# Turning the FFN's gated products by transposing DMAs, and splitting weight units in one piece

## The chip, the cores and the metric

The kernel runs on one core of a Trainium2 chip. The metric is the device time of one execution in microseconds (us). Before the change the median of three runs is 935.49 us (934.88 to 937.68). Engines are named as in the profile: PE multiplies matrices, DVE and ACT work on vectors, POOL does a few small things, SP issues the DMAs.

## The reference, cut to what matters

The program is a trunk of two layers over 256 tokens with 1024 channels in fp32. Each layer has a mixing part (gated linear attention beside grouped-query attention), then a SwiGLU feed-forward network (FFN), then an embedding step. The part that the change touches is this:

```python
gate, up = jnp.split(rms_norm(h, g_ffn_pre) @ w_ffn_in, 2, axis=-1)   # 256 x 2816 each
h = h + rms_norm((jax.nn.silu(gate) * up) @ w_ffn_out, g_ffn_post)
```

The gated product `silu(gate) * up` has 2816 columns. It is the left operand of the second product, so it has to stand with its columns on the partitions: it must be turned (transposed) before PE can use it.

## The kernel before, in words

**Precision.** Every fp32 operand of a matmul is split into a high and a low part of type fp32r, and a product is three matmuls, high by high, high by low, low by high (`mm3`, line 96; `times`, line 536, has the same three). A matmul takes 128 rows of contraction and 512 columns.

**Weights.** They come as *units* of four 128x512 blocks (2048 columns; 2112 in the first projection), in one fixed order, `plan`. `Stream` (line 208) loads a unit by a DMA on SP's queue into a buffer of the pool `raw` (two buffers), splits it into `wh` and `wl` (four buffers each) and hands it out in order. `fill` splits ahead as long as fewer than `depth` (4, for a while 3) units are held; `take` hands out the oldest of the list `ready`; `done` gives a unit back, starts the next load and splits the next unit. `put` (line 263) cuts a unit into `parts` pieces, by default two of 1024 columns, and `split` (line 108) does each piece with one ACT cast for the high part and one DVE subtraction for the low part.

**The FFN.** The 2816 columns are 11 blocks of 256. Blocks 0 and 1 are done for each half of the tokens at the start (four gated products of 128x256 in all, from line 1224). Blocks 4, 5 and 10 (`PLAIN`) are done one by one (`block`, line 1239; 128 tokens x 256 columns for both halves of the tokens, side by side in one 128x512 tile). Blocks 2 and 3, 6 and 7, 8 and 9 (`PAIRS`) are done by a scheme of seven products in place of eight (`seven`, line 575; each product takes one unit and 12 matmuls); it ends in two gated products of 128x512, one for each half of the tokens. Units of the pairs lie in lent `wh`/`wl` buffers, and DVE adds units to one another between the products (`step`, line 283). The second product is interleaved with all that: the string `FFN` gives the order, where u is a unit of a plain block, o a step of the second product (`out_step`), a digit a step of a pair. What is left of the second product follows at the end.

**The turning.** A gated product lies in a tile of the pool `t512` (five buffers of 128x512). After some *ticks* (a tick is counted after every six matmuls of the stream), PE transposes its 128x128 blocks against an identity into a PSUM bank, and `hid.put` splits the bank into high and low parts by an ACT cast and a DVE subtraction. `turned` (line 1215, by way of `transpose_in`, line 398) does this for the start and the pairs, `turn` in `block` (line 1253) for the plain blocks. The ticks to wait are `WAIT_FFN` 4, `WAIT_PAIR` 9, and `WAIT_LAST` 3 and 4 for the last pair.

**Order of the work.** Engines take their instructions in order. The order on each engine is made when the program is built, by a planner that goes by the order in which the instructions are written and by priorities (`high_priority` moves instructions forward). A `Task` (line 332) is a generator that runs to its first `yield` when it is made, and further when its ticks are over or when somebody needs its result (`need`). So what stands before the first `yield` is written out at once.

Of the kernel before, what the change touches and what calls it, by code (L numbers as in the profile page):

```python
# [10 lines left out]
F32 = mybir.dt.float32  # L11
F32R = mybir.dt.float32r
BF16 = mybir.dt.bfloat16
AF = mybir.ActivationFunctionType
ALU = mybir.AluOpType
AX = mybir.AxisListType

P = 128
T = 256
# [4 lines left out]

AHEAD, EMPTY, EMPTY_FIRST = 400, 100, 1600

WAIT, WAIT_FIRST, WAIT_NEXT, WAIT_H, WAIT_FFN, WAIT_MIX = 6, 4, 9, 5, 4, 3
# [10 lines left out]
PLAIN, PAIRS = (4, 5, 10), (2, 6, 8)  # L38
OUT = (0, 1, 2, 3, 4, 5, 10, 6, 7, 8, 9)

WAIT_PAIR, WAIT_LAST = 9, (3, 4)
UNIT = 2112
RQ = ((0, 288), (288, 672), (672, 1056))
C_GQ, C_GK, C_GV, C_GG, C_RA = 0, 512, 1024, 2048, 3072
# [4 lines left out]
def trunk_kernel(ctx: ExitStack, tc: tile.TileContext, a: dict, out: bass.AP):  # L49
# [58 lines left out]
    def split(hi, lo, src):  # L108

        nc.scalar.copy(hi, src)  # L110
        vsub(lo, src, hi.bitcast(F32))
# [96 lines left out]
    class Stream:  # L208
# [152 lines left out]
    class Split:  # L361
# [418 lines left out]
    for l in range(DEPTH):  # L780
# [458 lines left out]
        def block(b):  # L1239
            sg = t512()  # L1240
            o = [acc(), acc()]
            for kh in range(2):
                w = ws.take()
                for hf in range(2):
                    amode(o[hf], u2, hf, kh * 4, w, kh == 0, kh == 1)
                ws.done()
                if kh == 1:
                    for hf in range(2):
                        c = slice(hf * 256, (hf + 1) * 256)
                        nc.scalar.activation(sg[:, c], o[hf][:, 0:256], AF.Silu)  # L1250
                        vmul(sg[:, c], o[hf][:, 256:512], sg[:, c])

                    def turn():
                        yield WAIT_FFN
                        ps = aux()
                        for k in range(2):
                            for hf in range(2):
                                nc.tensor.transpose(
                                    ps[:, k * T + hf * P : k * T + (hf + 1) * P],
                                    sg[:, hf * 256 + k * P : hf * 256 + (k + 1) * P], ident,  # L1260
                                )
# [174 lines left out]
```

## Time and profile before

| | |
|---|---|
| median of the runs | 935.49 us (934.88 to 937.68) |
| span of the profiled execution, first to last instruction | 937.3 us |
| own time of the profiled execution outside its span | not given by the page; the span itself lies in the range of the runs |
| granted PE clock | 0.999 of full speed |
| PE busy | 922.6 us, 4697 matmuls and transposes |
| DVE busy | 732.4 us |
| ACT busy | 561.6 us |
| DMA | 169.26 MB, 52.8% of the 16 DMA engines' time |
| the FFN stages | about 271 to 442 us (first layer) and 729 to 902 us (second) |

How to read it: a row of the grouped views names the line, the engine, the operation, what it writes and reads by the program's names, its shape and how often it came; then the busy time in us, the mean in ns, and what ended the idle time before it. PEld is the load of PE's stationary operand, which goes on beside the matmuls. Names carry the part of the program (`0ffnin`: the FFN of the first layer). Matmuls are pipelined, so the listed length of one (some 390 ns) is longer than the distance from one to the next.

### The profile page before, as it was taken

Reading aid. Unit: us, or ns where it says so; the run is one execution under the profiler, and the core shown is the slowest. Engines: PE = TensorE matmul, PEld = TensorE weight load, DVE = VectorE, ACT = ScalarE, POOL = GpSimd, SP = SyncE. Lnnn points to the kernel's source line nnn. Section 1 sums busy time; section 2 is a strip of 40 time slices with the busy share of each in tenths; the row PEclk is TensorE's granted clock in tenths of the full one; section 3 lists DMA queues with packets and bytes.
Section 4 is the critical chain, followed back from the end, with each engine's and each line's share of the span. In section 5 each row is a group of like instructions: output and inputs, shape, how many; then the busy total and the mean of one; then the engine's idle time right before and its main releaser. Section 6 shows DMA issues by size and latency. Waiting matters only on the chain.

```text
span 937.3 us, 12331 instructions
## 1 busy us (share of the span) xinstructions
PE 922.6 (98%) x4697; PEld 783.9 (84%) x4697; DVE 732.4 (78%) x933; ACT 561.6 (60%) x928; POOL 80.8 (9%) x150
## 2 busy tenths in 40 slices
PE   8999999999999999999999999999999999999996
PEld 6998888888878878888899988888888788888786
DVE  4798978456569899999689799674666798989874
ACT  4669676443457565567666686754435666656563
POOL 3400214000000000000022001200001000000000
PEclk9999999999999999999999999999999999999999
DMA  6464455665275565547455525365553937463551
GB/s 229 168 223 137 136 191 191 191 213 180 91 249 169 203 233 190 203 143 249 167 175 181 192 78 180 116 244 181 200 190 103 310 114 268 154 266 112 180 180 45
DMA packets 88089, 169.26 MB, mean 181 GB/s; under 512 B 3351, under 2 KB 26391, under 8 KB 88030
## 3 DMA queue, kind: packets, MB, share of 16 engines
q1 hardware_dynamic: 88030, 168.47, 52.8%
q8 instruction: 37, 0.61, 0.3%
q14 instruction: 22, 0.18, 0.1%
HBM read 167.41 MB, written 1.05 MB: 180 GB/s over the span
## 4 chain that ended last, share of the span: by engine, by line
PE 79%; DVE 9%; DMA 4%; ACT 3%; issue 3%; POOL 1%; SPq 0%; POOLq 0%; ACTq 0%; DVEq 0%
PE acc_1ffnin L94 9%; PE acc_0ffnin L94 8%; PE acc_0gate L94 5%; PE acc_1gate L94 5%; PE acc_1merge L94 5%; PE acc_0merge L94 5%; PE acc_0ffnin L543 4%; PE acc_1ffnin L543 4%; PE acc_1gqk L94 2%; PE acc_0rq L94 2%; PE acc_0gqk L94 2%; PE acc_1ple L94 2%; PE acc_0gg L94 2%; PE acc_1gg L94 2%; PE acc_1v L94 2%
## 5 line engine op out<-in xcount | busy, mean ns | idle before, releaser
L94 PE MATMUL acc_1ffnin<-wh_1ffnin,big_1ffnin 128*128 128x512 f32 x176 | 56.9, 393 | 0.0
L94 PE MATMUL acc_0ffnin<-wh_0ffnin,big_0ffnin 128*128 128x512 f32 x176 | 56.8, 392 | 0.0
L110 ACT CAST wh_1ffnin<-raw_1ffnin 128x1024 fp32r<-128x1024 f32 x38 | 38.1, 1050 | 23.1 <-PE acc_1ffnin L94 7.7
L110 ACT CAST wh_0ffnin<-raw_0ffnin 128x1024 fp32r<-128x1024 f32 x38 | 37.9, 1049 | 22.0 <-PE acc_0ffnin L94 7.9
L106 DVE TENSOR_TENSOR wl_1ffnin<-raw_1ffnin,wh_1ffnin 128x1024 fp32r<-128x1024 f32 x38 | 44.8, 1219 | 5.6 <-ACT wh_1ffnin L110 5.4
L106 DVE TENSOR_TENSOR wl_0ffnin<-raw_0ffnin,wh_0ffnin 128x1024 fp32r<-128x1024 f32 x38 | 44.7, 1219 | 3.9 <-ACT wh_0ffnin L110 3.9
L94 PEld LDWEIGHTS acc_1ffnin<-wh_1ffnin,big_1ffnin 128*128 128x128 f32 x176 | 33.0, 188 | 7.1 <-ACT big_1ffnin L110 0.4
L94 PEld LDWEIGHTS acc_0ffnin<-wh_0ffnin,big_0ffnin 128*128 128x128 f32 x176 | 33.0, 188 | 6.7
L106 DVE TENSOR_TENSOR wl_0ffnin<-lent_0ffnin,wh_0ffnin 128x1024 fp32r<-128x1024 f32 x30 | 35.5, 1218 | 1.9 <-ACT wh_0ffnin L110 1.7
L106 DVE TENSOR_TENSOR wl_1ffnin<-lent_1ffnin,wh_1ffnin 128x1024 fp32r<-128x1024 f32 x30 | 35.4, 1218 | 2.0 <-ACT wh_1ffnin L110 2.0
L110 ACT CAST wh_1ffnin<-lent_1ffnin 128x1024 fp32r<-128x1024 f32 x30 | 30.2, 1049 | 9.0 <-PE acc_1ffnin L94 3.0
L110 ACT CAST wh_0ffnin<-lent_0ffnin 128x1024 fp32r<-128x1024 f32 x30 | 30.2, 1049 | 8.4 <-PE acc_0ffnin L94 3.7
L94 PE MATMUL acc_0ffnin<-wl_0ffnin,big_0ffnin 128*128 128x512 f32 x88 | 34.3, 389 | 0.0
L94 PE MATMUL acc_1ffnin<-wl_1ffnin,big_1ffnin 128*128 128x512 f32 x88 | 34.3, 389 | 0.0
L94 PE MATMUL acc_1ffnin<-wh_1ffnin,big_1wout 128*128 128x512 f32 x96 | 31.2, 394 | 0.0
L94 PE MATMUL acc_0ffnin<-wh_0ffnin,big_0wout 128*128 128x512 f32 x96 | 31.2, 394 | 0.0
L543 PE MATMUL acc_0ffnin<-wh_0ffnin,mid_0ffnin 128*128 128x512 f32 x96 | 31.0, 390 | 0.0
L543 PE MATMUL acc_1ffnin<-wh_1ffnin,mid_1ffnin 128*128 128x512 f32 x96 | 31.0, 390 | 0.0
L106 DVE TENSOR_TENSOR wl_0gate<-raw_0gate,wh_0gate 128x1024 fp32r<-128x1024 f32 x14 | 16.5, 1221 | 17.8 <-ACT wh_0gate L110 17.8
L106 DVE TENSOR_TENSOR wl_1gate<-raw_1gate,wh_1gate 128x1024 fp32r<-128x1024 f32 x14 | 16.5, 1221 | 17.8 <-ACT wh_1gate L110 17.8
L94 PE MATMUL acc_0rq<-wh_start,big_start 128*128 128x384 f32 (+1 forms) x96 | 25.4, 349 | 1.4 <-ACT big_start L120 1.4
L94 PE MATMUL acc_0gate<-wh_0gate,big_start 128*128 128x512 f32 x80 | 24.8, 389 | 0.0
(647 smaller groups left out, 2931.3 us busy)
## 6 DMA issues: line engine op xcount, KB each, us to landing
raw_0ffnin<-in_w_ffn_out_dram SPq DMA_DIRECT2D x11, 1024.0 KB, 5.3
raw_1ffnin<-in_w_ffn_out_dram SPq DMA_DIRECT2D x11, 1024.0 KB, 5.9
lent_0ffnin<-in_w_ffn_in_dram SPq DMA_DIRECT2D x6, 1024.0 KB, 8.7
lent_1ffnin<-in_w_ffn_in_dram SPq DMA_DIRECT2D x6, 1024.0 KB, 7.8
raw_0rq<-in_w_in_dram SPq DMA_DIRECT2D x4, 1024.0 KB, 5.2
raw_0v<-in_w_in_dram SPq DMA_DIRECT2D x4, 1024.0 KB, 5.0
raw_0gg<-in_w_in_dram SPq DMA_DIRECT2D x4, 1024.0 KB, 5.1
raw_0gate<-in_w_o_gla_dram SPq DMA_DIRECT2D x4, 1024.0 KB, 5.2
```

The lines of the kernel that those rows point to most:

```text
L94: return nc.tensor.matmul(o, lhsT, rhs, start=start, stop=stop)
L106: nc.vector.tensor_tensor(out=out, in0=in0, in1=in1, op=ALU.subtract)
L110: nc.scalar.copy(hi, src)
L543: nc.tensor.matmul(o, x, y, start=first and k + n == 0, stop=k == 3 and n == 2, skip_group_check=not first)
```

## The change

Two things change.

1. All gated products but those of the last pair are turned by a DMA. As a DMA transposes elements of two bytes, a fp32 tile is taken as two *planes* of 16-bit halves. `send` (new) takes two further tiles of `t512`, x and y: ACT copies the product to x with the halves sorted into two planes, and a transposing DMA on SP's queue turns all 128x128 blocks of x into y. `send` is called at once where the product is made; after `WAIT_PLANES`, 8 ticks, `join` runs: ACT copies y back to x with the halves joined to fp32, and `put` splits x as it split the PSUM bank before. `send_both` is the same for a plain block's tile with both halves of the tokens; its `join` has two copies of half the columns. The last pair goes on as before, with 3 and 4 ticks.

2. `put` of the weight stream has one piece of all columns in place of two, if the stream is open (always after the start) and at least one other unit stands in `ready`; else two pieces as before.

```diff
-        def put(self, x, parts=2):
+        def put(self, x, parts=None):
             ...
+            parts = parts or (1 if self.open and len(self.ready) > 1 else 2)
...
+        def send(self, src, k, n, hf):
+            x, y = (t512()[:, : n * P] for _ in range(2))
+            x16, y16 = x.bitcast(U16), y.bitcast(U16)
+            nc.scalar.copy(
+                x16.rearrange("p (s c) -> p s c", s=2), src.bitcast(U16).rearrange("p (c s) -> p s c", s=2)
+            )
+            nc.sync.dma_start_transpose(out=y16.rearrange("p (r t) -> p r t", t=P), in_=x16)
+            def join():
+                nc.scalar.copy(
+                    x16.rearrange("p (c s) -> p s c", s=2), y16.rearrange("p (s c) -> p s c", s=2)
+                )
+                self.put(x, k, n, hf * P, P)
+            return join
+
+        def send_both(self, src, k):
+            x, y = (t512() for _ in range(2))
+            ...
+            def join():
+                for i in range(2):
+                    nc.scalar.copy(
+                        x16.rearrange("p (k h t s) -> p h s k t", k=2, h=2, s=2)[:, i],
+                        y16.rearrange("p (s h k t) -> p h s k t", h=2, k=2, s=2)[:, i],
+                    )
+                self.put(x, k, 2, 0, T)
+            return join
...
-        def turned(src, k, n, hf, wait=WAIT_FFN):
+        def turned(src, k, n, hf, wait=None):
             def turn():
-                yield wait
-                transpose_in(hid, src, k, n, hf)
+                if wait in WAIT_LAST:
+                    yield wait
+                    transpose_in(hid, src, k, n, hf)
+                else:
+                    join = hid.send(src, k, n, hf)
+                    yield WAIT_PLANES
+                    join()
...
                     def turn():
-                        yield WAIT_FFN
-                        ps = aux()
-                        for k in range(2):
-                            for hf in range(2):
-                                nc.tensor.transpose(
-                                    ps[:, k * T + hf * P : k * T + (hf + 1) * P],
-                                    sg[:, hf * 256 + k * P : hf * 256 + (k + 1) * P], ident,
-                                )
-                        with tc.high_priority(AHEAD):
-                            hid.put(ps, 2 * b, 2, 0, T)
+                        join = hid.send_both(sg, 2 * b)
+                        yield WAIT_PLANES
+                        join()
...
-                turned(sg, 2 * b, 4, hf, WAIT_LAST[hf] if b == PAIRS[-1] else WAIT_PAIR)
+                turned(sg, 2 * b, 4, hf, WAIT_LAST[hf] if b == PAIRS[-1] else None)
```

More of the change, by code (lines that the diff above doesn't have):

```diff
@@ L13 @@
 BF16 = mybir.dt.bfloat16
+U16 = mybir.dt.uint16
 AF = mybir.ActivationFunctionType
@@ L25 @@
 AHEAD, EMPTY, EMPTY_FIRST = 400, 100, 1600
-WAIT, WAIT_FIRST, WAIT_NEXT, WAIT_H, WAIT_FFN, WAIT_MIX = 6, 4, 9, 5, 4, 3
+WAIT, WAIT_FIRST, WAIT_NEXT, WAIT_H, WAIT_MIX = 6, 4, 9, 5, 3
 W = dict(r=5, z=6, s0=4, s=3, s1=9, o0=1, o=1, k=4, q=3, a0=1, a1=4, a2=4, a3=1, g=6)
@@ L39 @@
 OUT = (0, 1, 2, 3, 4, 5, 10, 6, 7, 8, 9)
-WAIT_PAIR, WAIT_LAST = 9, (3, 4)
+WAIT_PLANES, WAIT_LAST = 8, (3, 4)
 UNIT = 2112
@@ L390, in put @@
             split(*self.at(k, n, t0, tn), src.rearrange("p (k t) -> p k t", t=tn))
+        def send(self, src, k, n, hf):
[13 more added lines that the diff above has]
+            x, y = (t512() for _ in range(2))
+            x16, y16 = x.bitcast(U16), y.bitcast(U16)
+            nc.scalar.copy(
+                x16.rearrange("p (s c) -> p s c", s=2), src.bitcast(U16).rearrange("p (c s) -> p s c", s=2)
+            )
+            nc.sync.dma_start_transpose(out=y16.rearrange("p (r t) -> p r t", t=P), in_=x16)
+            def join():
+                for i in range(2):
+                    nc.scalar.copy(
+                        x16.rearrange("p (k h t s) -> p h s k t", k=2, h=2, s=2)[:, i],
+                        y16.rearrange("p (s h k t) -> p h s k t", h=2, k=2, s=2)[:, i],
+                    )
+                self.put(x, k, 2, 0, T)
+            return join
         def tok(self, k, hf):
```

## The prediction

> **What bounds the kernel now.** I read the page's busy times first, then the stretches of the two FFN stages, then who PE waited for.
>
> ```profile
> PE 922.6 (98%) x4697; PEld 783.9 (84%) x4697; DVE 732.4 (78%) x933; ACT 561.6 (60%) x928; POOL 80.8 (9%) x150
> ```
>
> ```profile
> core 0: us, PE busy (x) PEld busy (x) DVE busy (x) ACT busy (x) POOL busy (x), PEclk, DMA share, GB/s
> 271.00:442.00 171.00, 170.17 (x775) 140.23 (x776) 155.37 (x155) 105.19 (x135) 1.82 (x3) 1.00 0.58 202
> 729.00:902.00 173.00, 171.18 (x779) 140.45 (x779) 155.78 (x156) 106.30 (x139) 0.86 (x2) 1.00 0.58 202
> ```
>
> ```profile
> 357.37 5.44 PE acc_0ffnin L543 x24
> ```
>
> The stages are PE's: it idles 0.8 us in the first FFN and 1.8 us in the second. Busy is only what the profile models, so I look at the rate too: in the chain of waits 24 matmuls take 5.44 us, 0.227 us each, and they keep that distance for long stretches. DVE comes next with 91% (155.4 of 171), ACT has 62% (105.2) and the DMA engines 58%. So work taken from PE shows in the time, as long as DVE, ACT and the loads keep up with a slightly faster PE.
>
> **What is removed.** Each layer has four gated products of two 128x128 blocks, three plain tiles of four, and six pair products of four: 44 transposes. The last pair keeps its eight, so 36 go, 72 in all.
>
> ```profile
> L402 PE MATMUL aux_0ffnin<-ident,t_0ffnin x32: 270/272/273, 273.8 to 430.2; 128*128 128x128 f32 x32
> L1258 PE MATMUL aux_0ffnin<-ident,t_0ffnin x12: 270/272/332, 302.3 to 348.5; 128*128 128x128 f32 x12
> ```
>
> ```profile
> 343.71 0.44 PE aux_0ffnin L402 x4
> ```
>
> The rows confirm 32 + 12 = 44. The listed 272 ns of one is pipelined; in the chain four take 0.44 us, 0.11 us each. 72 x 0.11 = **7.9 us** less of PE. Also the waits for the product that is to be turned go:
>
> ```profile
> PE aux_1ffnin L402 <- DVE t_1ffnin L103: 1.5, 1, 1.5
> PE acc_0ffnin L543 <- DVE mid_0ffnin L582: 0.6, 1, 0.6
> PE acc_0ffnin L94 <- DVE wl_0wout L106: 0.4, 2, 0.2
> PE acc_1rq L94 <- DVE wl_0ple L106: 0.4, 1, 0.4
> PE acc_1ffnin L94 <- DVE wl_1wout L106: 0.2, 1, 0.2
> PE aux_1ffnin L1258 <- DVE t_1ffnin L103: 0.2, 1, 0.2
> PE acc_0kv L94 <- DVE wl_0rq L106: 0.2, 1, 0.2
> ```
>
> The 1.5 us one belongs to the second layer's last pair, which stays (the chain has four such transposes at 884.88 us, quoted below). Only the 0.2 us one surely goes; the 0.6 us one is DVE being late, and DVE gets lighter (below). I take **0.5 us**, between 0.2 and 2.3.
>
> **What ACT gets.** No row shows a copy of 16-bit elements. The nearest are casts of fp32 from SBUF:
>
> ```profile
> 289.42 0.61 ACT L110 CAST mid_0ffnin<-t_0ffnin 128x512 fp32r<-128x512 f32 x1
> ```
>
> ```profile
> L110 ACT CAST wh_0ffnin<-raw_0ffnin 128x1024 fp32r<-128x1024 f32 x38 | 37.9, 1049 | 22.0 <-PE acc_0ffnin L94 7.9 <-DMA raw_0ffnin<-in_w_ffn_out_dram 3.8 <-issue 3.0
> L106 DVE TENSOR_TENSOR wl_0ffnin<-raw_0ffnin,wh_0ffnin 128x1024 fp32r<-128x1024 f32 x38 | 44.7, 1219 | 3.9 <-ACT wh_0ffnin L110 3.9
> L287 DVE TENSOR_TENSOR lent_0ffnin<-lent_0ffnin,lent_0ffnin 128x2048 f32<-128x2048 f32 x3 | 6.9, 2285 | 0.0
> ```
>
> A 512-column fp32 tile is 1024 elements of 16 bits. By element count a copy costs 1.05 us, a half one 0.61. If ACT goes by bytes, a 1024-element copy costs 0.61; if the stride of two costs a pass more, 2.1. I take the element count. Per layer: four small sends with two copies of 512 elements, 4 x 1.22 = 4.9; three plain tiles with one copy of 1024 and two of 512, 3 x 2.27 = 6.8; four pair products with two copies of 1024, 4 x 2.10 = 8.4. Sum 20.1 us (11 to 40 by the two ends).
>
> **What the whole pieces give back.** From 512 and 1024 columns, a cast costs 0.17 us plus 0.86 ns a column, so one of 2048 is 1.93 us against 2.10 for two. DVE's sum of 2048 columns, 2.285 us, stands for the subtraction: against 2 x 1.219 it saves 0.153. The stream finds `ready` empty only where all held units are out (the first projection, the two blocks at the FFN's start), so of 85 units a layer some 80 are whole, some 35 of them split in the FFN. There ACT saves 6.0 us and DVE 5.4. DVE ends at 150.0 of the 167 us that PE then needs (90%, as now); ACT at 105.2 + 20.1 - 6.0 = 119.3 (71%). By throughput both still hide behind PE, so I cost them at nothing; at 40 us of copies ACT has 139.
>
> **What ACT waits for.** The new plane copy stands behind the DVE multiply of the same product:
>
> ```profile
> 289.15 0.37 ACT L1233 ACTIVATE t_0ffnin<-acc_0ffnin 128x256 f32<-128x256 f32 x1
> 291.57 0.41 DVE L103 TENSOR_TENSOR t_0ffnin<-acc_0ffnin,t_0ffnin 128x256 f32<-128x256 f32 x1
> ```
>
> From the end of the Silu (289.52) to the end of the multiply (291.98) are 2.5 us; with nothing else between, ACT stands still that long, and the weight casts behind it with it. 11 x 2.5 = 27 us a layer, so ACT is taken for 147 of 167. The cover is the four held units, worth 2.72 to 5.44 us of PE each. The join waits for the DMA, but 8 ticks are 8 x 6 x 0.227 = 10.9 us after the product; `out_step` needs a pair's columns a round later. If that cover goes, every late cast becomes DVE's wait, then PE's, at the worst the 27 us a layer. Buffers: each send holds two of the five `t512` tiles until its join, the two sends of a pair four of them, so the send of a plain tile that follows waits for the first join; its columns too are needed a round later, so I cost this at nothing.
>
> **Where whole pieces come late.** PE takes units as they become ready after the stage changes (the four `wl` waits above). There a whole piece comes later by half a subtraction, 1.15 us, to half a cast more, 2.0 us; where the cast was ready long before, by nothing. Four places, 0 to 8 us; I take half a microsecond each, since one unit is always in hand: **+2.0 us**.
>
> **The transposing DMAs.** 11 a layer join SP's queue, in order with the weight loads; if one waits 2.5 us for its copy, the loads written behind it wait too. No row has a transposing DMA.
>
> ```profile
> out_dram<-h SPq DMA_DIRECT2D x3, 256.0 KB, 3.1
> h<-in_x_dram SPq DMA_DIRECT2D x4, 256.0 KB, 6.6
> raw_0ffnin<-in_w_ffn_out_dram SPq DMA_DIRECT2D x11, 1024.0 KB, 5.3
> ```
>
> ```profile
> DMA packets 17419, 34.92 MB, mean 203 GB/s; under 512 B 707, under 2 KB 6786, under 8 KB 17411
> q1 hardware_dynamic: 17411, 34.81, 57.8%
> ```
>
> A tile is 256 KB. By the plain rows it lands in 3.1 us. By packets: the stage's are 2.0 KB on average, so a 1 MB load is some 520 packets in 5.3 us, and 256 KB in rows of 256 bytes are 1024 packets, 10.6 us. I take 4 us, close to the plain row, since all data lie in SBUF and 256 KB is the quantity known. Seven large and four half ones are nine: 36 us of the 72 us a layer in which the DMA engines are free (42% of 171). A cost arises where a load is itself what PE's chain waits for:
>
> ```profile
> 312.60 4.94 DMA raw_0ffnin<-in_w_ffn_in_dram
> ...
> 321.52 5.38 DMA raw_0ffnin<-in_w_ffn_in_dram
> ...
> 870.82 6.41 DMA raw_1ffnin<-in_w_ffn_out_dram
> ...
> 884.88 0.66 PE aux_1ffnin L402 x4
> ```
>
> Even there PE hardly stood still (0.8 us in that whole stage). I cost the queue at nothing here and keep the price for the rival.
>
> The Trainium skill, page "VectorE: DVE Perf Modes", section "The three transpose paths", speaks against the change: it lists 390 ns for a 128x128 transpose on TensorE and 1309 ns by DMA, and advises TensorE where a PSUM destination will do. This case's trace has 0.11 us of PE time for the former; for the latter no run here has a row. Its page "DMA: Bandwidth & Descriptors", section "Latency and other measured facts", gives transposing DMAs 261 GB/s; an estimate from that is 1 us of movement a tile, by which the sum stays as it is.
>
> **Sum.** -7.9 - 0.5 + 2.0 = **-6.4 us** (0.7%). Against the profiled span of 937.3 us that is 930.9. The page gives no time outside the span, and the span is itself 1.8 us above the median of the runs, 935.49; the difference carries over, so I forecast **929.1 us**. Its own range: -9.4 (idle 1.5, nothing late) to -3.0, 926 to 932.5.
>
> **Rivals.** *B, the gain is given back at the stage changes.* All four places cost the full 2.0 us: +8.0 against -8.4, 935 us. For it: these are the places where DVE ends last. Against: DVE gets 5.4 us lighter in the FFN, and a unit in hand covers 2.7 us.
>
> *C, slower: the transposing DMAs hold up weight loads.* Place: the three loads above, and their likes in the FFN of both layers. A transposing DMA that stands before such a load, or shares the DMA engines with it, delays it by its own length. At 5.3 us (the row of a load) three loads cost 15.9 us: -8.4 + 2.0 + 15.9 = +9.5, 945 us. It decides from some 2.1 us per load (6.4 / 3). At 10.6 us a tile, nine tiles are 95 us against 72 free: 23 us a layer short, 935.5 - 6.4 + 46 = 975 us. For it: the DMA engines work in bursts, and the buffers `raw` are two. Against: SP mostly waits for a buffer, not the DMA engines for SP. The figure of the Trainium skill's page "VectorE: DVE Perf Modes", section "The three transpose paths", taken as if the 16-bit blocks went one after another, gives the estimate 8 x 1.309 = 10.5 us for a tile, the same end.
>
> *D, more than the sum.* Lighter DVE (some 12 us a layer over all stages, 80 x 0.153) also takes the other waits away; -8.4 - 2.5 = 924.6 us. Against: all interior waits together are hardly more.
>
> *E, little is turned by DMA or few units whole:* the code leaves no such way; a chance near nothing.
>
> **How the numbers follow.** A has 0.57, B 0.16, C 0.21, D 0.06. About 0.3%, 2.8 us, is what a measurement of this kernel can tell from no change. Faster by more: A but for a small part at its slow end, and D: 0.62. Within: most of B, that part of A, the mild end of C: 0.17. Slower: 0.21. The range reaches from D's edge, 923, into C, 942; left out are the upper half of C and a little of D.
>
> **What would show it.** Right: rows at the two transposing lines with 8 transposes a layer in place of 44, PE's count 72 lower, casts and subtractions of 2048 columns at 1.9 and 2.3 us, the FFN stages some 4 us shorter each, transposing DMAs landing in 3 to 5 us, joins that hardly wait. B would show as longer waits of PE for `wl` after the stage changes. C as weight loads issued or landing later and PE idle in the FFN behind ACT casts that waited for a load or a plane. The prediction is wrong if PE's idle time in an FFN stage grows by over 4 us, or if a plane copy costs ACT 2 us or more.

## The result, and the profile after

| | median of the runs | span of the profiled execution |
|---|---|---|
| before | 936.22 us (934.88 to 937.68) | 937.3 us |
| after | 958.88 us (956.74 to 960.69) | 957.9 us |

The ratio is 1.0227, with a 95% interval from 1.0211 to 1.0244. The forecast was 929.1 us in a range from 923 to 942; by the medians the change costs 22.7 us (by the ratio 21.3) where it was to gain 6.4.

First the busy times on the page of the kernel after:

```profile
PE 922.6 (96%) x4625; PEld 777.2 (81%) x4625; DVE 723.0 (75%) x771; ACT 586.6 (61%) x816; POOL 86.8 (9%) x150
```

The change did what it says. PE has 72 instructions fewer. DVE has 162 fewer (933 to 771), one for every unit that is now subtracted in one piece. But the span is 20.6 us longer with the same 922.6 us of PE's busy time, so by the page all of the 20.6 us is PE idle (that the busy time did not fall with the transposes is in part a lower clock, shown at the end).

The FFN stages, in the same stretches as before, counted from each stage's first matmul (the columns are the length, then busy time and instructions of each engine, the granted clock, the share of the DMA engines and GB/s):

```profile
core 0: us, PE busy (x) PEld busy (x) DVE busy (x) ACT busy (x) POOL busy (x), PEclk, DMA share, GB/s
273.80:452.00 178.20, 169.95 (x749) 136.90 (x748) 153.25 (x116) 120.39 (x120) 2.12 (x3) 1.00 0.65 203
742.80:922.40 179.60, 170.99 (x750) 137.24 (x749) 152.20 (x115) 122.17 (x125) 1.95 (x3) 1.00 0.66 203
```

PE idles 8.3 and 8.6 us here (178.20 - 169.95, 179.60 - 170.99), where it idled 0.8 and 1.8. So the two FFN stages hold some 14 of the 20.6 us. The DMA engines rose from 0.58 to 0.65. ACT rose from 105 to 120, nowhere near full, and DVE's busy time even fell by 2 to 4 us.

Who PE waited for, over the whole span (us in total, times, the longest):

```profile
PE acc_0ffnin L95 <- DVE wl_0ffnin L107: 4.3, 4, 1.6
PE acc_1ffnin L95 <- DVE wl_1ffnin L107: 4.3, 4, 1.7
PE acc_0ffnin L95 <- ACT wh_0ffnin L111: 2.9, 3, 1.3
PE acc_1ffnin L95 <- ACT wh_1ffnin L111: 2.5, 3, 1.3
PE aux_0ple L440 <- DVE mid_0ple L498: 2.4, 2, 2.2
PE acc_0ffnin L95 <- DVE wl_0wout L107: 2.4, 2, 1.8
PE acc_0kv L95 <- DVE wl_0rq L107: 2.0, 1, 2.0
PE acc_1ffnin L95 <- DVE wl_1wout L107: 1.7, 2, 1.2
```

Two kinds of wait stand here. The upper four lie inside the FFN and had no counterpart of that size before: PE waits for the low part of a unit (`wl`) and for its high part (`wh`). The others stand at changes of stage; at the three with `wl` the waits were 0.2 to 0.4 us before. PE waits for split units in both, so I looked at the splitting and at what else ACT and DVE do in the first FFN (busy us, mean ns of one, and what ended the idle time before):

```profile
L107 DVE TENSOR_TENSOR wl_0ffnin<-raw_0ffnin,wh_0ffnin 128x2048 fp32r<-128x2048 f32 x19 | 43.3, 2289 | 12.5 <-ACT wh_0ffnin L111 12.5
L111 ACT CAST wh_0ffnin<-raw_0ffnin 128x2048 fp32r<-128x2048 f32 x19 | 36.0, 1911 | 21.7 <-DMA raw_0ffnin<-in_w_ffn_out_dram 12.0 <-issue 2.8 <-DMA raw_0ffnin<-in_w_ple_proj_dram 2.4
...
L404 ACT COPY t_0ffnin<-t_0ffnin 128x1024 uint16<-128x1024 uint16 x4 | 5.4, 1357 | 0.1
L422 ACT COPY t_0ffnin<-t_0ffnin 128x512 uint16<-128x512 uint16 x6 | 4.2, 778 | 0.0
L398 ACT COPY t_0ffnin<-t_0ffnin 128x1024 uint16<-128x1024 uint16 x4 | 4.2, 1046 | 7.4 <-DVE t_0ffnin L104 7.4
L415 ACT COPY t_0ffnin<-t_0ffnin 128x1024 uint16<-128x1024 uint16 x3 | 3.2, 1059 | 1.0 <-DVE t_0ffnin L104 1.0
L404 ACT COPY t_0ffnin<-t_0ffnin 128x512 uint16<-128x512 uint16 x4 | 3.1, 778 | 3.4 <-DMA t_0ffnin<-t_0ffnin 3.4
L398 ACT COPY t_0ffnin<-t_0ffnin 128x512 uint16<-128x512 uint16 x4 | 2.5, 618 | 3.1 <-DVE t_0ffnin L104 3.1
```

DVE's subtraction of `raw` units idles 12.5 us behind ACT's casts; the same group idled 3.9 us before. The prices of single instructions are close to the forecast (2.289 against 2.285 us for a subtraction, 1.911 against 1.93 for a cast), and the copies add up to 22.6 us a layer (2.5 + 4.2 + 3.2 + 3.1 + 5.4 + 4.2). The sizes were right, and still the time is not there.

The transposing DMAs (KB are not given for them; the last number is the median us from issue to landing, over those whose landing the trace shows), and the load of a unit beside them:

```profile
t_0ffnin<-t_0ffnin SPq DMA_TRANSPOSE x11, 6.9
t_1ffnin<-t_1ffnin SPq DMA_TRANSPOSE x11, 7.5
raw_0ffnin<-in_w_ffn_out_dram SPq DMA_DIRECT2D x11, 1024.0 KB, 5.8
```

And the page's line on packets, first of the kernel before, then of the kernel after:

```profile
DMA packets 88089, 169.26 MB, mean 181 GB/s; under 512 B 3351, under 2 KB 26391, under 8 KB 88030
DMA packets 107222, 173.94 MB, mean 182 GB/s; under 512 B 22487, under 2 KB 45527, under 8 KB 107166
```

The trace shows the landing of only two transposing DMAs in each layer, at 6.8 and 6.9 us and at 6.5 and 8.6 us, for at most 256 KB; a weight load of four times the size takes 5.8. The 22 transposing DMAs bring 19,133 packets (107222 - 88089), practically all of them small.

### The profile page after: what moved, and what is told of

It reads as the page before. It is cut to its first block, busy times and chain, and to the rows that moved or that the text cites. A ratio compares the mean times of both kernels' runs of the same rounds, so it can differ in the third digit from the quotient of the medians.

```text
span 957.9 us, 11958 instructions
## 1 busy us (share of the span) xinstructions
PE 922.6 (96%) x4625; PEld 777.2 (81%) x4625; DVE 723.0 (75%) x771; ACT 586.6 (61%) x816; POOL 86.8 (9%) x150
## 2 busy tenths in 40 slices
DMA packets 107222, 173.94 MB, mean 182 GB/s; under 512 B 22487, under 2 KB 45527, under 8 KB 107166
## 3 DMA queue, kind: packets, MB, share of 16 engines
HBM read 167.41 MB, written 1.05 MB: 176 GB/s over the span
## 4 chain that ended last, share of the span: by engine, by line
PE 59%; DVE 15%; ACT 9%; DMA 9%; issue 5%; POOL 2%; SPq 0%; POOLq 0%; DVEq 0%; ACTq 0%
PE acc_1ffnin L95 5%; DVE wl_0ffnin L107 5%; PE acc_0gate L95 5%; PE acc_1gate L95 5%; PE acc_1merge L95 5%; PE acc_0merge L95 5%; DVE wl_1ffnin L107 3%; PE acc_1ffnin L581 3%; PE acc_0gqk L95 2%; PE acc_0rq L95 2%; PE acc_1ple L95 2%; PE acc_1gg L95 2%; PE acc_0gg L95 2%; PE acc_0v L95 2%; PE acc_0ffnin L95 2%
## 5 line engine op out<-in xcount | busy, mean ns | idle before, releaser
L107 DVE TENSOR_TENSOR wl_0ffnin<-raw_0ffnin,wh_0ffnin 128x2048 fp32r<-128x2048 f32 x19 | 43.3, 2289 | 12.5 <-ACT wh_0ffnin L111 12.5
L107 DVE TENSOR_TENSOR wl_1ffnin<-raw_1ffnin,wh_1ffnin 128x2048 fp32r<-128x2048 f32 x19 | 43.3, 2289 | 10.8 <-ACT wh_1ffnin L111 10.8
L111 ACT CAST wh_1ffnin<-raw_1ffnin 128x2048 fp32r<-128x2048 f32 x19 | 36.0, 1911 | 23.4 <-DMA raw_1ffnin<-in_w_ffn_out_dram 14.2
L111 ACT CAST wh_0ffnin<-raw_0ffnin 128x2048 fp32r<-128x2048 f32 x19 | 36.0, 1911 | 21.7 <-DMA raw_0ffnin<-in_w_ffn_out_dram 12.0
L107 DVE TENSOR_TENSOR wl_0ffnin<-lent_0ffnin,wh_0ffnin 128x2048 fp32r<-128x2048 f32 x15 | 34.2, 2287 | 5.1 <-ACT wh_0ffnin L111 4.8
L107 DVE TENSOR_TENSOR wl_1ffnin<-lent_1ffnin,wh_1ffnin 128x2048 fp32r<-128x2048 f32 x15 | 34.2, 2288 | 5.0 <-ACT wh_1ffnin L111 4.8
L111 ACT CAST wh_0ffnin<-lent_0ffnin 128x2048 fp32r<-128x2048 f32 x15 | 28.7, 1915 | 6.4 <-DVE lent_0ffnin L295 3.2
L111 ACT CAST wh_1ffnin<-lent_1ffnin 128x2048 fp32r<-128x2048 f32 x15 | 28.6, 1909 | 5.7 <-DVE lent_1ffnin L295 2.9
L107 DVE TENSOR_TENSOR wl_0gate<-raw_0gate,wh_0gate 128x2048 fp32r<-128x2048 f32 x7 | 16.1, 2293 | 19.1 <-ACT wh_0gate L111 19.1
L107 DVE TENSOR_TENSOR wl_1gate<-raw_1gate,wh_1gate 128x2048 fp32r<-128x2048 f32 x7 | 16.0, 2293 | 19.1 <-ACT wh_1gate L111 19.1
```

Of the source, the lines that this page charges most:

```text
L107: nc.vector.tensor_tensor(out=out, in0=in0, in1=in1, op=ALU.subtract)
```

## The experiments

Every ratio is to the kernel before, run on the same chip beside it. Ratios across chips are compared as ratios; 0.001 is 0.94 us.

**The two parts by themselves.** The first kernel keeps the turning by DMA and undoes the whole pieces; the second does the opposite.

```diff
 # after, with
-            parts = parts or (1 if self.open and len(self.ready) > 1 else 2)
+            parts = parts or 2
```

> The changed kernel with every weight unit split in two pieces as before: the transposing DMAs alone. Theory Q (the transposing DMAs stand in SP's queue and hold up weight loads; also their plane copies take ACT) says that most of the 21 us is theirs: 947 to 956 us, with the loads to the lent buffers at the start of each FFN still issued 5 to 6 us late. Theory W (one piece of 2048 columns comes later than the first of two pieces, and PE, DVE and ACT wait for one another longer) says that without it the gain that was forecast for PE appears: 927 to 934 us.

```diff
 # before, with
-        def put(self, x, parts=2):
+        def put(self, x, parts=None):
+            parts = parts or (1 if self.open and len(self.ready) > 1 else 2)
```

> The kernel before with weight units split in one piece as in the change, all turning by PE as before: the pieces alone. Theory Q: 935 to 942 us, the cost outside the FFN stages only (about 6.5 us between the stage starts of the two profiles). Theory W: 945 to 958 us, with waits of PE for wl of 1 to 2 us in the FFN too.

With two pieces the turning by DMA takes 936.86 us against 937.66, a ratio of 0.9992 [0.9980, 1.0005]: no difference. One piece alone takes 957.39, 1.0211 [1.0194, 1.0229], 19.7 us. So nearly the whole loss hangs on the second, smaller-looking part of the change, and the first part gains nothing either.

Who waited in the kernel with one piece and no DMA, PE first, then DVE:

```profile
PE aux_1ffnin L1259 <- DVE t_1ffnin L103: 3.4, 1, 3.4
PE aux_0ffnin L1259 <- DVE t_0ffnin L103: 2.4, 1, 2.4
PE acc_0ffnin L94 <- DVE wl_0wout L106: 2.2, 2, 1.7
PE acc_0kv L94 <- DVE wl_0rq L106: 2.0, 1, 2.0
```

```profile
DVE wl_1ffnin L106 <- ACT wh_1ffnin L110: 21.9, 18, 5.3
DVE wl_0ffnin L106 <- ACT wh_0ffnin L110: 21.5, 16, 5.3
```

The second view again, of the kernel before:

```profile
DVE wl_1ffnin L106 <- ACT wh_1ffnin L110: 11.6, 13, 4.2
...
DVE wl_0ffnin L106 <- ACT wh_0ffnin L110: 9.8, 10, 4.2
```

With two pieces DVE may begin a unit when the first half is cast (1.05 us); with one piece it waits for the whole cast (1.91 us), and its idle time behind ACT doubles from 10 to 22 us a layer. What PE then waits for is not only a unit: it is DVE's multiply for the plain block (`t`), which stands in DVE's order behind the late work.

Behind both of these long waits, which end at 350.4 and 820.6 us, the clock of PE falls (the last three columns are the granted clock, the DMA share and GB/s):

```profile
348.00:352.00 4.00, 1.63 (x7) 1.28 (x7) 4.00 (x5) 1.90 (x1) 0.00 (x0) 0.80 0.04 14
352.00:356.00 4.00, 4.00 (x18) 3.23 (x17) 2.28 (x3) 1.24 (x3) 0.00 (x0) 0.77 0.46 113
820.00:824.00 4.00, 3.38 (x13) 2.75 (x14) 3.70 (x5) 0.59 (x1) 0.00 (x0) 0.68 0.00 0
824.00:828.00 4.00, 4.00 (x18) 3.32 (x17) 0.69 (x1) 2.39 (x2) 0.00 (x0) 0.89 0.94 306
```

Taken as half speed beside full speed, these are 3.4 us at half speed in each layer, and each costs some 1.7 us. The kernel before has no such stretch. So the loss of this kernel is made of PE's waits and of a slower clock after the longest of them.

The loads come later as well, since a load needs the buffer that a subtraction frees: in the first FFN ACT's casts wait 11.4 us for their loads in place of 3.8, in the second 8.8 in place of 7.5. That alone is not the loss, because the kernel with copies and no DMA (below) has 11.3 and 13.4 us of these waits and is faster than the kernel before. No run gives the pool `raw` a third buffer, so the part of the late loads isn't measured by itself.

The stage lengths, from the first matmul on `acc_ffnin` to the first on `acc_emb`, divide the loss:

| | first FFN | second FFN | between them |
|---|---|---|---|
| before | 181.7 | 182.4 | 277.0 |
| after | 189.0 | 189.0 | 280.8 |
| two pieces, DMA | 182.4 | 179.8 | 277.1 |
| one piece, no DMA | 187.1 | 187.5 | 282.9 |

In its profiled execution (955.2 us, 17.9 over that of before) one piece costs 5.4 + 5.1 us in the FFNs and the other 7.4 outside. The waits for `wl_0wout` (2.2 us) and `wl_1wout` (1.5) come at the start of the FFN stages as they are counted here. Over the waits of the kernel before (0.4 and 0.2) they are 3.1 of the 10.5 us, which leaves 7.4 for the rest of the two FFNs.

**Which half of the splitting is it?** One kernel casts in two pieces and subtracts in one, the other the reverse; both turn by PE. (The few units that the rule leaves in two pieces are cut once more here.)

```diff
 # the rule of one piece, split by
+            m = src.shape[-1] // 2
+            for c in (slice(0, m), slice(m, 2 * m)):
+                nc.scalar.copy(hi[:, c], src[:, c])
+            vsub(lo, src, hi.bitcast(F32))
```

> Kernel before, PE turns; a unit that the change would split in one piece is cast in two pieces of 1024 columns and subtracted in one of 2048. Theory D (with one piece DVE starts a unit a whole cast late, and DVE is the engine that PE follows): DVE still waits for the whole unit's cast: 950 to 960 us, near the 957 us of one piece. Theory A (the long cast blocks the short work behind it on ACT): 936 to 943 us. Theory V (the long subtraction blocks short work on DVE and comes late to PE): 950 to 960 us.

```diff
+            m = src.shape[-1] // 2
+            nc.scalar.copy(hi, src)
+            for c in (slice(0, m), slice(m, 2 * m)):
+                vsub(lo[:, c], src[:, c], hi[:, c].bitcast(F32))
```

> Kernel before, PE turns; a unit that the change would split in one piece is cast in one piece of 2048 columns and subtracted in two of 1024. Theory D: DVE again starts a unit a whole cast late, 948 to 960 us. Theory A: 948 to 960 us. Theory V: 936 to 943 us. So D leaves both mixed kernels slow, A mends only the one with two casts, V only this one.

They take 953.54 us, 1.0139 [1.0107, 1.0171], and 953.82 us, 1.0153 [1.0123, 1.0184]: 13.0 and 14.4 us by the ratios. Each keeps some two thirds to three quarters of the 19.7, so cutting one of the two instructions alone doesn't bring the overlap within the unit back. What the two share with the whole piece is that DVE begins a unit only once all of it is cast; they differ from it in that PE gets a first half early, of the high part in the one and of the low part in the other. How much belongs to which is not settled. If the three effects add, DVE's late start is 7.7 us (13.0 + 14.4 - 19.7), the long cast 6.7 and the long subtraction 5.3, and each of the three ratios is uncertain by 1.6 to 3 us. The falls of the clock are part of it: the first kernel takes 948.80 us in its run at a mean clock of 0.998 and 956.05 in that at 0.992, the second 949.50 and 956.00.

**Is it that DVE has no slack?** If so, taking other work from DVE should shrink the loss. Here the additions of weight units to one another are left out, 24 of them (the page counts 933 against 909; my expectation said 36), once with two pieces and once with one.

```diff
 # step, at n = 1, 2, 3 and 5
-                nc.vector.tensor_tensor(out=x.raw[:, c], in0=x.raw[:, c], in1=z.raw[:, c], op=ALU.add)
```

> The kernel before with DVE's additions of weight units to one another left out (the four of `step`; the pairs' seven products then take wrong weights; nothing else changes). It takes some 36 additions of 1024 or 2048 columns from DVE. Theory D (DVE sets the pace in the FFN where it is 90% busy): this kernel by itself is the base; PE has the same matmuls, so at most 0 to 4 us are gained: 931 to 938.

> The same additions left out, and units in one piece (as in e2_one_piece_pe_turn). Theory D: with DVE no longer near its limit the FFN hardly feels the late start of a whole subtraction; what is left over the kernel with two pieces and no additions is what lies outside the FFN, 9 us or less, and the FFN stages differ by under 1.5 us each (5 in e2). Rival L (whole pieces are late whatever DVE's load): the difference stays at 18 to 22 us and the FFN stages differ by some 5 us each.

With two pieces 934.57 us, 0.9966 [0.9953, 0.9979]; with one 947.38, 1.0099 [1.0073, 1.0126]. The difference is 12.5 us where it was 19.7. The FFN stages of the two, first the one with two pieces, then the one with one piece:

```profile
270.50:441.00 170.50, 169.97 (x775) 140.38 (x776) 130.86 (x145) 106.53 (x137) 1.82 (x3) 1.00 0.58 205
728.50:899.00 170.50, 170.31 (x778) 140.65 (x778) 130.51 (x144) 105.97 (x137) 0.86 (x2) 1.00 0.58 205
```

```profile
270.50:441.00 170.50, 169.22 (x769) 139.05 (x770) 125.66 (x103) 101.36 (x94) 2.90 (x5) 1.00 0.57 201
728.50:899.00 170.50, 167.74 (x761) 137.00 (x760) 124.40 (x100) 101.97 (x94) 1.57 (x2) 1.00 0.57 197
```

DVE is busy 77% (130.86 of 170.5) in place of 91%. The FFN stages are 181.3 and 180.0 us with two pieces and 182.5 and 183.4 with one: the loss there falls from 10.5 us to 1.2 + 3.4 = 4.6. The waits at the stage's start stay (2.0 us for `wl_0wout`, 1.7 for `wl_1wout`; 0.5 and 0.2 with two pieces), so they hold 3.0 of these 4.6 us, and the rest of the FFNs falls from 7.4 to 1.6. There the long waits for the multiply are gone (0.7 us in the second layer, none in the first), and with them the falls of the clock. So the loss within the FFN hangs on DVE's load. One thing besides the load changes with it: a summed unit's cast no longer follows an addition, and these runs don't part the two. The first FFN behaves as that theory said (under 1.5 us), the second doesn't. Of the 10.1 us between the two profiled spans (934.4 and 944.5) 5.5 are left outside the FFN, where neither kernel leaves work out; with the additions they were 7.4. And relieved of 50 us of work (732.4 to 681.8), DVE gives PE only 3.2 us with two pieces: it was not the bound before, merely the next one.

**Is it the units after a change of stage?** Here one piece is used only where four units stand ready, which was to let a stage begin with halves.

```diff
-            parts = parts or (1 if self.open and len(self.ready) > 1 else 2)
+            parts = parts or (1 if self.open and len(self.ready) > 3 else 2)
```

> The kernel before with one piece only where four units stand in `ready`, so after each stage change, and where the depth is 3, units come in two pieces. If the part outside the FFN comes from whole pieces right after a change of stage, that part (about 9 of 20 us) goes and the FFN's stays: 948 to 951. If the FFN's part too comes from the first units of the stage, 938 to 943. If the place of the whole units doesn't matter: 955 to 958.

946.26 us, 1.0084 [1.0058, 1.0111], 7.9 us. My expectation had the wrong part disappear. 60 units are whole now (ACT has 868 instructions against 928), 12 of them among the FFN's own 38 `raw` units, and the FFN stages are 183.2 and 182.3 us, 1.5 over and 0.1 under those of before: the FFN's loss went, since few whole units are left there. The stretch between the FFNs stays at 284.0, 7.0 us over. Half of it (3.5) lies at one place, where PE waits 1.8 us for ACT's cast of an operand. That cast stands behind a unit's, which waited 3.5 us for its load, and the clock then falls (below): lateness in splitting comes back as a late load, since a load needs the buffer that the subtraction frees. The edit did not reach every change of stage: whole units are left at `wl_0rq`, and PE still waits 1.3, 1.2 and 1.3 us for `wl_0rq`, `wl_0wout` and `wl_1wout` (0.2, 0.4 and 0.2 before). So this run doesn't say what the late units of the stage changes cost, only that the outer part holds other stalls too.

**What the turning itself is worth.** With two pieces, I took it apart: the first kernel leaves the 72 transposes out of the kernel before and splits the gated products as they lie; the second has the copies of the change, but no DMA and no turning.

```diff
 # before, with
-                transpose_in(hid, src, k, n, hf)
+                hid.put(src, k, n, hf * P, P)          # all but the last pair; plain blocks alike
```

> The kernel before (two pieces) with the 72 transposes left out and nothing in their place: the gated products are split as they lie, at the same ticks, so the second product of the FFN multiplies untransposed blocks. What PE alone can gain. If PE bounds the FFN (theory P, as predicted), before minus 7.9 us or a little more: 928 to 931 us. If DVE bounds it as much (theory B), before minus 0 to 4 us: 934 to 938 us.

```diff
 # after in two pieces, with
-            nc.sync.dma_start_transpose(out=y16.rearrange("p (r t) -> p r t", t=P), in_=x16)
+                                                        # the join copies x to y, and y is split
```

> DMA turning with two pieces, but the transposing DMA left out: ACT makes the planes and joins them again untransposed, at the same ticks, so the second product multiplies untransposed blocks. Between e9 and this stand ACT's copies alone, between this and e1 (0.9992 of before) the DMAs alone. Theory C (copies and ACT's waits take the gain): close to e1, 935 to 939 us. Theory S (the DMAs in SP's queue and the joins that wait for them take it): close to e9, 928 to 932 us.

Without any turning 927.90 us against 937.87, 0.9898 [0.9881, 0.9915]; with the copies alone 932.00, 0.9937 [0.9922, 0.9952]. So the transposes on PE are worth 10.0 us, ACT's copies cost 4.1 (932.00 - 927.90; by the ratios the two are 9.6 and 3.7, and uncertain by 1.6 and some 2), and the DMAs eat the rest: from 0.9937 to 0.9992, 0.0055 or 5.2 us, which the two intervals leave uncertain by some 2 us. PE's waits name the DMAs' way of costing. In the kernel with DMAs and two pieces:

```profile
PE acc_0ffnin L95 <- DVE wl_0ffnin L107: 2.4, 3, 1.6
PE acc_1ffnin L95 <- DVE wl_1ffnin L107: 1.6, 3, 1.1
```

These two waits don't stand in the list of the kernel without DMAs, which has two others in the FFNs, of 1.4 and 1.2 us for `wh`. What lies ahead of them is, first, weight loads that stand behind transposing DMAs in SP's queue, and the cast that waits for such a load:

```profile
272.58 5.33 SPq L401 DMA_TRANSPOSE t_0ffnin<-t_0ffnin  x2
277.97 1.12 SPq L258 DMA_DIRECT2D lent_0ffnin<-in_w_ffn_in_dram  x2
287.41 1.05 ACT L111 CAST wh_0ffnin<-lent_0ffnin 128x1024 fp32r<-128x1024 f32 x1 [2.42 <-DMA lent_0ffnin<-in_w_ffn_in_dram]
```

Second, the chain of waits has a transposing DMA itself:

```profile
351.76 5.42 DMA t_0ffnin<-t_0ffnin
357.20 1.39 ACT t_0ffnin L422 x2
361.48 2.37 DVE wl_0ffnin L107 x2
```

The two transposing DMAs hold SP for 5.33 us, 2.8 of them a wait for the second product's copy. The loads behind them are issued 18.2 us after the stage's first matmul, against 16.5 in the kernel before and 16.3 in the kernel without DMAs, and the cast comes 2.6 us later than before within the stage. The load that the chain names takes 8.68 us, which is no delay: in the kernel before the median of these loads is 8.7. So they come late because they are issued late. The chain goes on from this cast, by DVE, to PE's longest wait in this kernel (1.6 us). At 351.76 the transposing DMA is itself in the chain, with the two copies that join its result and the subtraction that DVE could do only after them.

**Another place for the DMAs, the copies, or the joins.** Four kernels move one piece each: the DMAs to ACT's queue (with whole pieces), the copies to POOL, twelve ticks in place of eight, and the start's products and block 10 turned by PE (all three with two pieces).

```diff
-            nc.sync.dma_start_transpose(...)
+            nc.scalar.dma_start_transpose(...)
```

> The changed kernel with the transposing DMAs issued from ACT's queue instead of SP's, all else the same: no weight load stands behind one. ACT pays the issue, 22 times 1.2 us. Theory Q: the FFN stages get shorter, in all 940 to 950 us. Theory W: no gain, 957 to 965 us, since ACT only gets more to do.

```diff
-            nc.scalar.copy(...)             # the four plane copies
+            nc.gpsimd.tensor_copy(...)
```

> DMA turning with two pieces, and the plane copies and joins on POOL, idle for nine tenths of the time, in place of ACT. Theory C: ACT is as free as before, the 7.9 us of PE show, 927 to 932 us. Theory S: the DMAs stand in SP's queue as before, 934 to 940 us. If a copy on POOL takes several us or slows DVE beside it, 935 to 950 us, and the rows of POOL and DVE show it.

```diff
-WAIT_PLANES, WAIT_LAST = 8, (3, 4)
+WAIT_PLANES, WAIT_LAST = 12, (3, 4)
```

> DMA turning with two pieces and joins after 12 ticks (16 us) in place of 8 (11 us), all else as in e1. If joins that wait for their DMA on ACT are a good part of the loss: 931 to 935 us. If the loss is ahead of the join (planes behind the multiply, SP's queue), or tiles held longer cost as much: 936 to 942 us.

```diff
-                if wait in WAIT_LAST:
-                    yield wait
+                if wait in WAIT_LAST or n == 2:
+                    yield wait or 4
                     transpose_in(hid, src, k, n, hf)
 # and block 10 as in the kernel before
```

> DMA turning with two pieces, but the four products of the FFN's start (whose DMAs stand ahead of the loads to the lent buffers in SP's queue) and plain block 10 (whose join held ACT for its DMA at 357 us) are turned by PE as before: 24 transposes a layer... 36 less 12 = 24 stay with the DMAs, 48 in all, 5.3 us of PE. If these two places are where the gain went: 931 to 934 us. If the loss is spread (copies, DVE), no better than e1: 936 to 939 us.

On ACT's queue the kernel takes 977.80 us, 1.0425 [1.0409, 1.0442], 18.6 us more than after by the ratios; the three landings that the trace shows are 2.4, 9.5 and 9.9 us. With the copies on POOL 961.65, 1.0252 [1.0223, 1.0282], 24 us more than on ACT: by shape a copy takes 0.9 to 2.8 us there in the mean (the profiler's times on POOL are rough). ACT's split of the turned product then waits for POOL's copies (15.8 and 19.1 us for the joins at L404 alone), DVE waits for ACT, and PE waits 9.7 and 9.1 us for `wl` in the FFNs. With twelve ticks 938.82, 1.0013 [0.9999, 1.0027]: ACT's waits for the DMAs fall from 10.2 to 5.9 us, and those for the multiply grow. In the kernel with eight ticks and in that with twelve:

```profile
ACT t_0ffnin L398 <- DVE t_0ffnin L104: 3.3, 4, 1.5
```

```profile
ACT t_0ffnin L398 <- DVE t_0ffnin L104: 10.0, 5, 3.6
```

The later joins put the copies at places where DVE's multiply is the late one. With the start and block 10 on PE 941.27, 1.0042 [1.0027, 1.0057], a miss: fewer DMAs are worse, by two stalls of 2.3 and 1.7 us for `wl` that weren't there, each with a fall of the clock behind it. The order of the work shifts by a few us with every edit, and a stall of that size weighs as much as what was to be saved.

**Copies with PE's transposes.** Two kernels have all copies of the change and no DMA, and let PE turn the joined tile, with whole pieces and with two.

```diff
-            nc.sync.dma_start_transpose(out=y16.rearrange("p (r t) -> p r t", t=P), in_=x16)
-                self.put(x, k, n, hf * P, P)
+                transpose_in(self, y, k, n, hf)
```

> The changed kernel with its plane copies, ticks, tiles and one-piece units, but no transposing DMA: x is joined back on ACT into y and PE turns y as before (72 transposes, 7.9 us of PE come back). What differs from the changed kernel is the DMA alone. Theory Q (SP): without the DMAs the loads are on time, 945 to 952 us although PE has more to do. If instead ACT's copies and their wait for the multiply are the cost, or the pieces (W), it stays at 958 to 967 us.

> The kernel before (two pieces, PE turns) with the plane copies, joins, ticks and tiles of the change, but no transposing DMA: x is joined back on ACT into y and PE turns y. Theory C (the change's turning gains 7.9 us on PE and ACT's copies, with ACT's waits for the multiply, take the same back): before plus 6 to 10 us, 943 to 948 us. Theory S (the copies are hidden and the DMAs' place in SP's queue takes it back): 936 to 940 us, as before.

968.30 us, 1.0327 [1.0311, 1.0342], and 956.50 us, 1.0189 [1.0173, 1.0205]. They were to price the copies, and don't, since PE now stands in order behind the join:

```profile
PE aux_0ffnin L447 <- ACT t_0ffnin L408: 6.9, 1, 6.9
PE aux_1ffnin L447 <- ACT t_1ffnin L408: 6.5, 1, 6.5
```

That is a wait that neither kernel of the change has, and 13.4 of the 17.7 us of the second kernel. The price of the copies is taken from the two kernels without turning above.

No version beats the kernel before: the best that computes the whole is the turning by DMA with two pieces, and it is no faster.

## Why the prediction was wrong

**The step that failed** is "What the whole pieces give back", with its "By throughput both still hide behind PE, so I cost them at nothing", and the +2.0 us of "Where whole pieces come late". Together they stood for +2.0 us; measured alone it is +19.7. The sum took ACT and DVE as two amounts of work, each below PE's. They are a chain: DVE's part of a unit begins when ACT's piece ends, and a whole piece makes ACT's lead 0.86 us longer (1.91 against 1.05) and DVE's single step 1.07 us longer (2.29 against 1.22). With DVE busy to 90% these delays reached PE; with DVE relieved the FFN's loss fell from 10.5 to 4.6 us, of which 3.0 are waits at the stage's start. DVE's saving of 5.4 us a layer turned into idle time: it waited 10 to 12 us a layer more for ACT. Nor had the sum a term for the clock: two stretches at half speed cost another 1.7 us each in the kernel with one piece alone.

**The stage changes.** Rival B named them and priced them at 8.0 us at most. Its mechanism is seen at three of its four places in the kernel with one piece alone: 2.0 us for `wl_0rq`, 2.2 and 1.5 for the two `wl_wout`. These are 5.7 us (0.8 before), so its price holds. They lie partly within the FFN stages, and the loss goes far beyond them: B was wrong in holding that nothing else would be lost. No rival had the FFN's lost overlap as its mechanism.

**PE bounds.** -7.9 and -0.5 us: right. Without the transposes 10.0 us go (8.0 to 11.2 by the interval of the ratio), so the 8.4 lie within what was measured.

**ACT's copies cost nothing.** Wrong by 4.1 us. Their amount was right (20.1 forecast, 22.6 measured), and the plane copies cost what a fp32 cast of as many elements costs; only the join is dearer (1.36 us for 1024 elements, 0.78 for 512). The cover was wrong: ACT is busy 68% in the FFN of the kernel after (120.39 of 178.20), but its casts stand in line behind a copy that waits for DVE or for a DMA. The wait for the multiply was forecast at up to 27 us a layer and is 11.5 and 9.8 in the kernel after (10.5 and 8.8 at L398, 1.0 each at L415).

**The transposing DMAs cost nothing.** Wrong by some 5 us. I chose 4 us to the landing, by the kilobytes; the few landings that the traces show are 6.5 to 8.6 after and 5.4 and 7.0 with two pieces, between that row and the 10.6 us of the count of packets. The count itself was right: rows of 256 bytes make 18,432 packets, and 19,133 came. Rival C's mechanism exists, as loads issued 1.7 us late behind transposing DMAs in the first FFN, not as loads that take longer; the DMAs' whole cost, joins that wait for them included, is a third of its 15.9 us.

**How the terms add up.** -10.0 (transposes) + 4.1 (copies) + 5.2 (DMAs) + 19.7 (whole pieces) = +19.0, against 22.7 by the medians and 21.3 by the ratio. So 2.3 us are left over by the ratios (19.8 for one piece alone, -0.8 for the DMAs with two pieces), within the some 2.5 us that the three intervals together leave. Whole pieces and late joins may cost something by meeting on the same two engines; no run takes that meeting apart. Of the 7.4 us outside the FFN in the kernel with one piece alone, the list of PE's waits names 5.5: 1.8 more for `wl_0rq`, 2.8 for operands of the second layer's attention (`aux_1at`), 1.1 more at `aux_0ple` and 0.9 at `acc_0ple`, less 1.1 at two places where before waited longer. The rest is open.

The slow end of the prediction's own range, -3.0 us, isn't worked out from its terms; its own most pessimistic terms, all four stage changes at 2.0 us, come to -0.4.

**The signs the prediction named.** Its own condition for being wrong, PE's idle time in an FFN stage growing by over 4 us, was met twice (8.3 against 0.8, 8.6 against 1.8). That the copies stay under 2 us was met. That joins hardly wait was not: the small ones wait 3.4 and 5.3 us a layer for their DMA.

## What to carry to other kernels

Where two engines work on a unit one after the other, the size of the piece is the length of the pipeline's step: fewer and larger pieces save a fixed cost per instruction (0.15 us here) and lose the overlap within the unit, which counts as soon as the second engine is near its limit: with DVE at 91% in the FFN whole pieces cost 19.7 us, with DVE at 77% 12.5. Before costing work on a second engine at nothing because its busy share has room, look at what stands in order behind it, and whether it is itself waiting for somebody. And when two edits come as one, price them apart: here the first was worth nothing and the second cost nearly everything.

## What the runs showed of the hardware that I had not expected

**A short stall of PE can halve its clock for a while.** The granted clock of the kernel after at the 2.0 us wait for `wl_0rq`, in narrow stretches:

```profile
46.00:48.00 2.00, 0.57 (x2) 0.49 (x3) 2.00 (x3) 0.07 (x1) 2.00 (x1) 1.00 0.01 4
48.00:49.00 1.00, 1.00 (x4) 0.80 (x3) 1.00 (x1) 0.00 (x0) 0.08 (x1) 0.64 0.48 49
49.00:50.00 1.00, 1.00 (x4) 0.78 (x3) 1.00 (x2) 0.00 (x0) 0.00 (x0) 0.50 0.86 283
50.00:51.00 1.00, 1.00 (x4) 0.81 (x3) 0.70 (x3) 0.00 (x0) 0.00 (x0) 0.50 1.03 401
51.00:52.00 1.00, 1.00 (x4) 0.77 (x4) 0.00 (x0) 0.17 (x1) 0.00 (x0) 0.66 1.07 387
52.00:53.00 1.00, 1.00 (x6) 0.82 (x5) 0.51 (x2) 0.46 (x4) 0.37 (x2) 1.00 0.99 381
```

After the stall the clock is 0.50 for 3.4 us (0.72 + 1 + 1 + 0.68 us at half speed by the four rows), which costs another 1.7 us. From the first matmul on `acc_0kv` to the first on `acc_0v` this kernel takes 3.9 us more than the kernel before, the sum of the two within 0.2 us. The kernel with one piece and no DMA has the same 2.0 us wait with no fall of the clock, and takes 2.3 us more there; its two falls stand behind the waits of 2.4 and 3.4 us shown above. Between its start and its end the kernel before has no such fall, nor have the five others in two pieces whose time is within 0.2% of it or below; the kernel after has two, the two mixed kernels three and two, and the two with the copies ahead of PE's transposes have longer stretches at 0.50. The shortest single stall with a fall right behind it is 1.7 us, in the kernel with the start and block 10 on PE; in the kernel with two casts and one subtraction two stalls of 1.2 and 0.9 us, 2.1 us apart, have one behind them. Within one execution the falls stand on a grid: the two of the kernel after begin 447.1 us apart and the two of the kernel with one piece 471.0, which is 131 and 138 times the 3.413 us that one of them lasts in the trace. The Trainium skill, page "TensorE: Matmul & The Clock Gate", section "Part 1: The HAM clock gate", tells of a clock at 4/8 after an idle window of about 3.4 us, by a window that runs freely. The half speed and the 3.4 us agree with these rows, and that the same stall is hit once and spared once, and the grid, fit a free window. That page of the Trainium skill advises, in its section "Why this matters for your kernels", no idle gaps of PE over some 3 us; that a stall of 1.7 to 2.0 us is enough here doesn't agree with it.

**Small transposing DMAs are slow to issue, and their landings spread.** SP is mostly held for 1.2 us by the issue of one, against 0.37 for a plain load. Most landings that the traces show take 5.4 to 8.6 us for at most 256 KB, with packets of which nearly all are under 512 B; in the kernel with only six of them a layer they go from 3.1 to 8.5, and from ACT's queue from 2.4 to 9.9. Each trace shows the landing of a few of them only.

**POOL copies 16-bit elements slowly:** by shape 0.9 to 2.8 us in the mean, for copies for which ACT takes 0.6 to 1.4. Its shortest copies of 512 elements take 0.61 us, as on ACT, so part of the longer ones is something other than the copy, and no run says what.
